# A hybrid encoder layer on one core: transfers of the block products moved to POOL's queue and to column tiles, and the attention's fill respread

## The chip, the cores and the metric

The kernel runs on one core of a Trainium2 chip. The core has TensorE (PE) for matmuls, VectorE (DVE), ScalarE (ACT), GpSimd (POOL) and SyncE (SP), which here only issues transfers. SP, ACT and POOL each have a queue of DMA issues of their own; all transfers are carried out by the same 16 DMA engines. Every engine works off its instructions in order. The metric is the time of one execution on the device in microseconds (us); less is better.

## The reference

One layer of a bidirectional hybrid encoder on a sequence of 512 positions with 2048 channels, in float32, then a final RMSNorm.

```
h = rmsnorm(x, norm_w)
u = h @ w_in            # columns: z_ssm | x,B,C | dt fwd, dt bwd | q_a | kv_a, kr | z_attn | g_ssm | g_attn
# branch A: conv + SiLU on x,B,C; chunked state-space scan forward and backward (chunks of 128,
#           32 heads of 64, 4 groups, state 128); y = (y_fwd + y_bwd + d_skip*x) * silu(z_ssm); group RMSNorm
# branch B: q = rmsnorm(q_a) @ w_uq; k, v = rmsnorm(kv_a) @ w_ukv; rotary part; 16 heads of 128,
#           softmax over all 512 positions; o = (p @ v) * silu(z_attn)
merged = sigmoid(g_ssm) * (y @ w_proj_ssm) + sigmoid(g_attn) * (o @ w_proj_attn)
out = rmsnorm(x + merged @ w_out, final_norm_w)
```

## The kernel before

Each float32 matmul is done as three matmuls of split operands (high and low part, type fp32r): high by high, high by low, low by high. Weights come in chunks of 128 partitions by 1024 (512 KB). A chunk is loaded by SP into one of three buffers `wraw` (`wchunk`, `w_load`, `w_tile("w")`), ACT copies the high part into `wh` (L163, L431), DVE subtracts to get the low part `wl` (L164, L432); `wh` and `wl` have three buffers each.

PE's instructions run in the order in which they are written. On the other engines and queues a scheduler that works from its own cost model orders them; `tc.high_priority(offset=n)` lets what is inside go as if it stood n instructions earlier (`AHEAD` is 60, `LOAD_AHEAD` 160). `tc.keep_in_program_order` pins an instruction behind what was written before it on its engine.

The stages, in order of time:

1. The input is normed and turned; the dt tile and six tiles of `xbc` of group 0 are computed (`xbc_gen`; 16 k-steps of three matmuls each, then a conv of width 4 and SiLU). `h_sums` makes the sums of quarters of h that the block products need, in pool `sx`. `dt_make` makes the time steps, stored to `dt_d`.
2. The products for `z_ssm`, `g_ssm` and `g_attn` (`wz`, `wgs`, `wga`) are block products with seven multiplications in place of eight (`Strassen`). Each of the two column pairs (`pair`) runs P1, P5, P6, P2, P3, P7, P4; a `product` is 4 chunks of 12 matmuls. P1 loads its columns into tiles X, P5 adds column block Y into X (`t2`), P6 uses that sum, P2 adds a further block (`t4`), P4 uses the result; P3 uses Y, P7 a further sum. After a product, hooks load (`L`) or split (`C`) the next operands, which go through `wraw` as `xraw`. The results, through silu or sigmoid, go to scratch (`zs_d`, `gs_d`, `ga_d`).
3. The state-space part, four groups (`ssd_group`). A group loads its BT, CT and four `xs` tiles from scratch, turns them, and runs states, off-diagonal and diagonal blocks. Between its small steps, `gap` runs matmuls of other tiles (xbc of the next group, qkv, z_attn) from a queue, `fill`; one unit of fill is one matmul of 512 columns. Tiles in pool `sw` have eight buffers of tag `t`; `dt64` is the first of them. In the background POOL's queue adds up weight blocks in DRAM (`t_jobs`: T1 and T3 of `wps`, `wpa`).
4. Attention, 16 heads. For a head: `scores` for four blocks of 128 queries, `trans` (turning the probabilities through TensorE), and `pv` for the head before. Between these run `unit`s of fill: first the q, k, v and rotary products of later heads (`qk_gen`, `rope_gen`, `v_gen`), then, queued at the end of head 14, `wps.head()`: P1 and P2 of both column pairs of `wps`. The sums of the attention output that the block products need (`sums(o_d, ...)`, `o_sums`) are DRAM-to-DRAM copies and accumulating transfers on POOL's queue; columns 0 to 1023 at head 12, the others in six steps hung on `wps`'s hooks.
5. The block products `wps` (operands y) and `wpa` (operands o), with summed weights T1 and T3 loaded from DRAM. In `wps` P1 and P2 are done by then, so a pair is P5, P6, P3, P7, P4, and a block of weights is added to X by `t4_alone`. `fetch_ps`/`fetch_pa` load gates (into tag `st`, three buffers) and the partial results of `wps` (`ms`); `done_ps` multiplies and stores `ms_d`, `done_pa` multiplies, adds and turns the result.
6. The last product with `w_out`, the residual, the final norm and the store.

Of the kernel before, what the change touches and what calls it, by code (L numbers as in the profile page):

```python
# [11 lines left out]
F32 = mybir.dt.float32  # L12
# [60 lines left out]
def build(tc, a):  # L73
# [320 lines left out]
    def xbc_gen(g, i, new):  # L394
        p_ = mm("xbc")
        yield from gemm_steps(p_, win(T_XBC + 6 * g + i), h_h, h_l)
        put(xbc_d[g][i], conv_silu(p_, (4 * g + i, 16 + g, 20 + g)[max(0, i - 3)], st("xbc"), new))
# [147 lines left out]
    def product(name, op, chunk, extra=None, pre=None):  # L545

        used.append((used[-1] + 1) % 4)
        bs = [b(name) for b in SETS[used[-1]]]
        for m in range(4):
            raw = chunk(m)  # L550
            h, l = w_split(raw)
            if extra:
                extra(m, raw)
            if pre and m == 2:
                pre()
            for i in range(2):
                for jj in range(2):
                    j = 2 * m + jj
                    xh, xl = op(0, j, i), op(1, j, i)
                    wh, wl = (t[:, jj * 512:(jj + 1) * 512] for t in (h, l))  # L560
                    pe.matmul(bs[i], xh, wh, start=(j == 0), stop=False)  # L561
                    pe.matmul(bs[i], xh, wl, start=False, stop=False)  # L562
                    pe.matmul(bs[i], xl, wh, start=False, stop=(j == 7))  # L563
            yield 12
        product_done()
        return bs

    class Strassen:


        def __init__(self, w, ops, r, done, fetch=None, hooks=None):
            self.w, self.ops, self.r, self.done = w, ops, r, done
            self.fetch, self.hooks = fetch or (lambda t, b: None), hooks or {}

# [41 lines left out]
        def pair(self, cp, headed=False):  # L616

            w, made = self.w, (self.w, cp, "T1") in t_d
            X, Y = [], []
            if not headed:  # L620
                def c1(m):
                    if made:
                        return w_load(w_tile("w"), w, cp, 0, 0, m)
                    X.append(w_load(w_tile("X"), w, cp, 0, 0, m))
                    return X[m]

                p1 = evict((yield from product("P1", self.op("x11"), c1, None if made else
                                               lambda m, raw: w_more(raw, w, cp, 0, 1, m))), "p1")
                self.hook(cp, "P1")
            else:  # L630
                p1 = self.p1[cp]

            def c5(m):
                if made:
                    X.append(t_load(w_tile("X"), w, cp, "T1", m))
# [19 lines left out]
            A = yield from product("P6", self.op("S2"), lambda m: X[m], t4_alone if headed else None)  # L655
# [15 lines left out]
            A = yield from product("P7", self.op("S3"), c7, None, self.pre(2, 2 * cp + 1))  # L671
# [80 lines left out]
    def h_back():  # L752
        h_ops.raws["x21"] = []
        for q in range(2):
# [46 lines left out]
    nc.sync.dma_start(dt64, dt_d)  # L801
# [42 lines left out]
    def ssd_group(g):  # L844
# [29 lines left out]
        nc.sync.dma_start(BT, xbc_d[g][4])  # L874
        nc.sync.dma_start(CT, xbc_d[g][5])
        xss = []
        for ct in range(4):
            xss.append(tmp2("xs"))
            nc.sync.dma_start(xss[ct], xbc_d[g][ct])
# [423 lines left out]
    def fetch_ps(t, b):  # L1303
        fetched[t, b] = st("gate")
        nc.sync.dma_start(fetched[t, b], gs_d[t][b])

    def fetch_pa(t, b):
        fetched[t, b] = st("gate")
        nc.sync.dma_start(fetched[t, b], ga_d[t][b])
        fetched["m", t, b] = sum_tile("ms")  # L1310
        nc.sync.dma_start(fetched["m", t, b], ms_d[t][b])

    def done_ps(t, b, o):
        dve.tensor_mul(o, o, fetched.pop((t, b)))
        nc.sync.dma_start(ms_d[t][b], o)
# [32 lines left out]
    o_half = sums(o_d, slice(1024, 2048))  # L1348

    def o_sums(n):  # L1350
        return lambda: [tc.keep_in_program_order(f()) for f in o_half[n]]
# [11 lines left out]
    def m_room(b):  # L1363
# [6 lines left out]
        (1, "P5"): [L(o_ops, "S1"), o_sums(5)], (1, "P6"): [C(o_ops, "S1"), L(o_ops, "S2")],  # L1370
        (1, "P3"): [C(o_ops, "S2"), L(o_ops, "S4")], (1, "P7"): [C(o_ops, "S4"), L(o_ops, "S3")],
        (1, "P4"): [C(o_ops, "S3"), L(o_ops, "x22")]})
    wpa = Strassen("wpa", o_ops, -1, done_pa, fetch_pa, {
        (0, "P1"): [C(o_ops, "x22")],
        (1, "P1"): [residual], (1, "P6"): [lambda: m_room(2), lambda: m_room(3)], (1, "P2"): [residual, m_load(0)],
        (1, "P3"): [m_split(0), m_load(1)], (1, "P7"): [m_split(1)]})

    for hd in range(AH):
# [4 lines left out]
        unit = 3 if hd < 12 else 2 if hd < AH - 1 else 7  # L1383
        early = unit if hd < AH - 1 else 0
        scores(hd, 0)
        if hd:
            fill.run(early)
            trans(hd - 1, 3)
        fill.run(2 * early)
        scores(hd, 1)  # L1390
        fill.run(3 * early)
        if hd:
            pv(hd - 1)
        if hd == 12:
            for step in sums(o_d, slice(0, 1024)):
                for f in step:
                    f()
        trans(hd, 0)
        scores(hd, 2)
        fill.run(3 * unit)  # L1400
        trans(hd, 1)
        fill.run(2 * unit)
        scores(hd, 3)
        fill.run(3 * unit)
        trans(hd, 2)
        fill.run(3 * unit)
        if hd == AH - 2:
            fill.all()
            close_pool("ap")
# [7 lines left out]
    fill.run(12)  # L1417
    trans(AH - 1, 3)
    fill.run(24)
# [4 lines left out]
    for w in ("S1", "S2"):  # L1424
        y_ops.raws[w] = [cols.tile([P, 1024], F32, tag="X", bufs=4, name="xraw") for q in range(2)]
        for q in range(2):
            nc.sync.dma_start(y_ops.raws[w][q], yn_d[w][:, q * 1024:(q + 1) * 1024])
        C(y_ops, w)()
    fill.all()
    L(y_ops, "S4")()  # L1430
    run(wps.pair(0, True))
# [154 lines left out]
```

## Time and profile before

| | |
|---|---|
| median of 3 runs | 2116.05 us (2115.52 to 2118.23) |
| the profiled execution | 2111.87 us, span 2110.1 us |
| mean granted TensorE clock | 0.975 |
| PE busy | 1979.2 us, 94% of the span |
| DVE, ACT, POOL busy | 70%, 45%, 13% |
| chain that ended last | PE 75%, DVE 10%, DMA 6%, issue 5%, ACT 2%, POOL 1% |
| DMA | 378.56 MB, mean 179 GB/s |

The profile is of one execution. A row of a group has the line, engine, operation, output and inputs, shapes, count, then busy time, mean duration, idle time of the engine before it and what ended it. In a row of waits stand who waited for whom, the sum, how often, and the longest. The granted clock is the share of full speed at which the throttle let TensorE run. Matmuls overlap, so the time of one is read from the distance of their starts.

### The profile page before, as it was taken

How to read it: one execution, taken by the hardware profiler on the slowest of the kernel's cores; microseconds unless marked ns; L12 is line 12 of the kernel's file. 1: busy time of each engine (PE TensorE's matmuls, PEld its weight loads, DVE VectorE, ACT ScalarE, POOL GpSimd, SP SyncE). 2: the span in 40 equal slices, each digit the busy share in tenths (PEclk: the TensorE clock that was granted, in tenths of full speed). 3: DMA queues.
4: the chain of work that ended last, by engine and by line, in shares of the span. 5: the costliest groups of instructions: out<-in, count | busy, mean ns of one | idle time of the engine just before them, and what ended most of it. 6: DMA issues, size and time to landing. Idle time of an engine off the chain costs nothing.

```text
span 2110.1 us, 24659 instructions
## 1 busy us (share of the span) xinstructions
PE 1979.2 (94%) x9074; PEld 1633.7 (77%) x9074; DVE 1467.0 (70%) x1946; ACT 958.6 (45%) x1344; POOL 275.1 (13%) x265
## 2 busy tenths in 40 slices
PE   6989999999989999899899999999988889979998
PEld 5878888888777777787788788888776768857886
DVE  7966676677669589798794767667667877755342
ACT  6444445444444545545555344444444444423232
POOL 0001010010042151342420011200100000000110
PEclk9999999999999999999999999999999999989999
DMA  5468657756646747587564867863659794744332
GB/s 192 143 182 201 168 126 186 191 127 161 169 156 187 216 125 212 189 230 217 156 195 157 240 169 185 226 158 87 166 187 307 247 307 139 268 150 144 109 121 80
DMA packets 170552, 378.56 MB, mean 179 GB/s; under 512 B 15872, under 2 KB 65152, under 8 KB 169856
## 3 DMA queue, kind: packets, MB, share of 16 engines
q1 hardware_dynamic: 113904, 255.11, 37.1%
q0 software_dynamic: 21696, 75.51, 17.8%
q10 hardware_dynamic: 34832, 46.38, 6.2%
q8 instruction: 71, 1.16, 0.2%
q14 instruction: 49, 0.40, 0.1%
HBM read 325.03 MB, written 98.04 MB: 201 GB/s over the span
## 4 chain that ended last, share of the span: by engine, by line
PE 75%; DVE 10%; DMA 6%; issue 5%; ACT 2%; POOL 1%; SPq 0%; ACTq 0%; DVEq 0%; POOLq 0%
PE P L562 11%; PE P L563 11%; PE P L561 11%; PE f L1456 3%; PE f L1454 3%; PE f L1455 3%; PE za L170 2%; PE za L168 2%; PE za L169 2%; PE xbc L168 2%; PE xbc L170 2%; PE xbc L169 2%; DVE sum L980 2%; DVE wl L164 1%; PE pb L1249 1%
## 5 line engine op out<-in xcount | busy, mean ns | idle before, releaser
L432 DVE TENSOR_TENSOR wl<-X,wh 128x1024 fp32r<-128x1024 f32 x144 | 175.5, 1222 | 86.5 <-ACT wh L431 85.9
L164 DVE TENSOR_TENSOR wl<-wraw,wh 128x1024 fp32r<-128x1024 f32 (+2 forms) x148 | 175.4, 1185 | 74.4 <-ACT wh L163 69.2
L431 ACT CAST wh<-X 128x1024 fp32r<-128x1024 f32 x144 | 151.4, 1054 | 162.6 <-PE P L563 145.2
L432 DVE TENSOR_TENSOR wl<-wraw,wh 128x1024 fp32r<-128x1024 f32 x98 | 120.6, 1231 | 148.1 <-ACT wh L431 146.3
L163 ACT CAST wh<-wraw 128x1024 fp32r<-128x1024 f32 (+2 forms) x150 | 145.4, 969 | 164.9 <-PE xbc L169 43.0
L431 ACT CAST wh<-wraw 128x1024 fp32r<-128x1024 f32 x98 | 103.2, 1053 | 203.7 <-PE f L1456 74.9
L561 PE MATMUL P<-wh,h_h 128*128 128x512 f32 x384 | 150.5, 392 | 5.4 <-ACT wh L431 5.4
L168 PE MATMUL xbc<-h_h,wh 128*128 128x512 f32 x384 | 152.3, 397 | 0.0
L562 PE MATMUL P<-wl,h_h 128*128 128x512 f32 x384 | 150.3, 391 | 0.5 <-DVE wl L432 0.5
L170 PE MATMUL xbc<-h_h,wl 128*128 128x512 f32 x384 | 150.3, 391 | 0.4 <-DVE small L827 0.4
L169 PE MATMUL xbc<-h_l,wh 128*128 128x512 f32 x384 | 150.2, 391 | 0.0
L563 PE MATMUL P<-wh,h_l 128*128 128x512 f32 x384 | 150.1, 391 | 0.0
L432 DVE TENSOR_TENSOR wl<-Y,wh 128x1024 fp32r<-128x1024 f32 x64 | 78.3, 1223 | 64.2 <-ACT wh L431 64.1
L561 PE MATMUL P<-wh,S 128*128 128x512 f32 x288 | 112.0, 389 | 0.0
L562 PE MATMUL P<-wl,S 128*128 128x512 f32 x288 | 112.0, 389 | 0.0
L563 PE MATMUL P<-wh,S 128*128 128x512 f32 x288 | 112.0, 389 | 0.0
L431 ACT CAST wh<-Y 128x1024 fp32r<-128x1024 f32 x64 | 67.4, 1054 | 91.2 <-PE P L563 83.3
L170 PE MATMUL za<-h_h,wl 128*128 128x512 f32 x256 | 101.1, 395 | 5.0 <-DVE wl L164 5.0
L168 PE MATMUL za<-h_h,wh 128*128 128x512 f32 x256 | 102.2, 399 | 0.0
L169 PE MATMUL za<-h_l,wh 128*128 128x512 f32 x256 | 100.7, 393 | 0.0
L561 PEld LDWEIGHTS P<-wh,h_h 128*128 128x128 f32 x384 | 72.6, 189 | 21.0 <-ACT wh L431 5.8
L170 PEld LDWEIGHTS xbc<-h_h,wl 128*128 128x128 f32 x384 | 72.5, 189 | 16.3 <-DVE small L827 0.8
(623 smaller groups left out, 5162.4 us busy)
## 6 DMA issues: line engine op xcount, KB each, us to landing
wraw<-wi SPq DMA_DIRECT2D x102, 512.0 KB, 4.2
da<-da_d SPq DMA_DIRECT2D x64, 256.0 KB, 4.3
T_wps<-wps POOLq DMA_DIRECT2D x32, 512.0 KB, 6.2
T_wpa<-wpa POOLq DMA_DIRECT2D x32, 512.0 KB, 9.7
wraw<-wo SPq DMA_DIRECT2D x32, 512.0 KB, 3.4
wraw<-wps SPq DMA_DIRECT2D x24, 512.0 KB, 4.1
wraw<-wpa SPq DMA_DIRECT2D x16, 512.0 KB, 5.2
xbc_d<-xbc ACTq DMA_DIRECT2D x24, 256.0 KB, 2.5
```

Of the source, the lines that this page charges most:

```text
L163: act.copy(h, raw)
L164: (dve if ahead[0] else pool).tensor_sub(l, raw, h.bitcast(F32))
L168: pe.matmul(out, wh, xh, start=start, stop=False)
L169: pe.matmul(out, wh, xl, start=False, stop=False)
L170: pe.matmul(out, wl, xh, start=False, stop=stop)
L431: act.copy(hi_, raw)
L432: dve.tensor_sub(lo_, raw, hi_.bitcast(F32))
L561: pe.matmul(bs[i], xh, wh, start=(j == 0), stop=False)
L562: pe.matmul(bs[i], xh, wl, start=False, stop=False)
L563: pe.matmul(bs[i], xl, wh, start=False, stop=(j == 7))
L1454: pe.matmul(acc, mh, wh, start=(start and k == 0), stop=False)
L1455: pe.matmul(acc, mh, wl, start=False, stop=False)
```

## The change

It has these parts.

- `xbc_gen` may run its conv in its output tile. Five tiles of group 0 run before the block products' pool is opened, the sixth after it and after the issue of the first X loads of `wz` (`first_columns`). The load of operand S3 moves from the hook after P1 to the hook after P5.
- The load of `dt64` is issued `LOAD_AHEAD`, those of BT, CT and `xs` `AHEAD`.
- In `pair`: where sums are made beforehand, P1 takes its weights through X tiles in place of `wraw`, and P7 its T3 through Y tiles. `t4_alone` moves from P6 to P7. For `wps` the first T1 loads are issued before the rest of the fill (`first_columns`).
- A product yields after every 3 matmuls in place of every 12.
- Gates, partial results and their stores (`fetch_ps`, `fetch_pa`, `done_ps`) go on POOL's queue in place of SP's.
- The late `o` sums are split in two halves of 512 columns; one is issued during heads 14 and 15 and before P5, the other on the hooks. Operand loads and splits on the hooks are moved, mostly by one product.
- Attention: `unit` is 2.8 for heads 0 to 13 and 2 for the last two, with what was run too much or too little carried over (`some`); before it was 3, 2 or 7. The head's products are queued in head 14 after `scores(14, 1)`. Operands S1 and S2 go through Y tiles, issued `LOAD_AHEAD`.

The diff, cut; in the heads' loop `fill.run(n)` becomes `some(n)` throughout, and the block `if hd == AH - 2` (close `ap`, load and split x11 and x12, queue `wps.head()`) stands after `scores(hd, 1)` and its fill in place of at the head's end:

```diff
@@ xbc_gen
-        put(xbc_d[g][i], conv_silu(p_, (4 * g + i, 16 + g, 20 + g)[max(0, i - 3)], st("xbc"), new))
+        o = st("xbc")
+        put(xbc_d[g][i], conv_silu(p_, (4 * g + i, 16 + g, 20 + g)[max(0, i - 3)], o, new or (lambda n: o)))
@@ product
-            yield 12
+                    yield 3
@@ Strassen
+            self.made = (w, 0, "T1") in t_d
+            self.ahead = {}
+        def first_columns(self, cp):
+            self.ahead[cp] = [self.columns(w_tile("X"), cp, m) for m in range(4)]
+        def columns(self, t, cp, m):
+            if self.made:
+                return t_load(t, self.w, cp, "T1", m)
+            return w_load(t, self.w, cp, 0, 0, m)
@@ pair
+            X, Y = self.ahead.pop(cp, []), []
+            def column(m):
+                if m == len(X):
+                    X.append(self.columns(w_tile("X"), cp, m))
+                return X[m]
-                    if made:
-                        return w_load(w_tile("w"), w, cp, 0, 0, m)
+                    "P1", self.op("x11"), (lambda m: w_load(w_tile("X"), w, cp, 0, 0, m)) if made else column,
             def c7(m):
-                return t_load(w_tile("w"), w, cp, "T3", m) if made else Y[m]
+                return t_load(w_tile("Y"), w, cp, "T3", m) if made else Y[m]
-            A = yield from product("P6", self.op("S2"), lambda m: X[m], t4_alone if headed else None)
+            A = yield from product("P6", self.op("S2"), lambda m: X[m])
-            A = yield from product("P7", self.op("S3"), c7, None, self.pre(2, 2 * cp + 1))
+            A = yield from product("P7", self.op("S3"), c7, t4_alone if headed else None, self.pre(2, 2 * cp + 1))
@@ before the gates' products
-    for i in range(6):
+    for i in range(5):
         run(xbc_gen(0, (4, 5, 0, 1, 2, 3)[i], sxt))
-    gates[0].hooks = {(0, "P1"): [lambda: h_ops.load("S3")],
-                      (0, "P5"): [lambda: [h_part("S3", 256, q) for q in range(2)]]}
+    gates[0].hooks = {(0, "P5"): [lambda: h_ops.load("S3"), lambda: [h_part("S3", 256, q) for q in range(2)]]}
+    gates[0].first_columns(0)
+    run(xbc_gen(0, 3, None))
@@ state-space part
-    nc.sync.dma_start(dt64, dt_d)
+    with tc.high_priority(offset=LOAD_AHEAD):
+        nc.sync.dma_start(dt64, dt_d)
-        nc.sync.dma_start(BT, xbc_d[g][4])
-        nc.sync.dma_start(CT, xbc_d[g][5])
...
+        with tc.high_priority(offset=AHEAD):
+            nc.sync.dma_start(BT, xbc_d[g][4])
+            nc.sync.dma_start(CT, xbc_d[g][5])
...
@@ fetch_ps, done_ps (fetch_pa in the same way)
-        nc.sync.dma_start(fetched[t, b], gs_d[t][b])
+        pool.dma_start(fetched[t, b], gs_d[t][b])
-        nc.sync.dma_start(ms_d[t][b], o)
+        pool.dma_start(ms_d[t][b], o)
@@ hooks
-    o_half = sums(o_d, slice(1024, 2048))
+    o_late = [sums(o_d, slice(1024 + 512 * i, 1536 + 512 * i)) for i in range(2)]
...
     wps = Strassen("wps", y_ops, -1, done_ps, fetch_ps, {
-        (0, "P5"): [C(y_ops, "S4"), L(y_ops, "S3"), o_sums(0)], (0, "P6"): [C(y_ops, "S3"), L(y_ops, "x22"), o_sums(1)],
-        (0, "P3"): [C(y_ops, "x22"), L(o_ops, "x11"), o_sums(2)],
-        (0, "P7"): [C(o_ops, "x11"), L(o_ops, "x12"), o_sums(3)], (0, "P4"): [C(o_ops, "x12"), o_sums(4)],
...
+        (0, "P5"): [C(y_ops, "S4"), L(y_ops, "S3"), o_sums(5, 0), o_sums(0)],
+        (0, "P6"): [C(y_ops, "S3"), L(y_ops, "x22"), o_sums(1)], (0, "P3"): [C(y_ops, "x22"), o_sums(2)],
+        (0, "P7"): [L(o_ops, "x11"), o_sums(3)], (0, "P4"): [C(o_ops, "x11"), L(o_ops, "x12"), o_sums(4)],
...
@@ attention
-        unit = 3 if hd < 12 else 2 if hd < AH - 1 else 7
-        early = unit if hd < AH - 1 else 0
+        unit = 2.8 if hd < AH - 2 else 2
...
-    fill.run(12)
+    some(8)
     trans(AH - 1, 3)
-    fill.run(24)
+    some(16)
     pv(AH - 1, pb)
@@ after attention
     for w in ("S1", "S2"):
-        y_ops.raws[w] = [cols.tile([P, 1024], F32, tag="X", bufs=4, name="xraw") for q in range(2)]
+        with tc.high_priority(offset=LOAD_AHEAD):
+            y_ops.raws[w] = [cols.tile([P, 1024], F32, tag="Y", bufs=4, name="xraw") for q in range(2)]
...
+        if w == "S1":
+            wps.first_columns(0)
         C(y_ops, w)()
     fill.all()
     L(y_ops, "S4")()
+    o_sums(4, 0)()
```

More of the change, by code (lines that the diff above doesn't have):

```diff
@@ L873, in ssd_group @@
             fill.until(("xbc", g))
-        nc.sync.dma_start(BT, xbc_d[g][4])
-        nc.sync.dma_start(CT, xbc_d[g][5])
         xss = []
-        for ct in range(4):
-            xss.append(tmp2("xs"))
-            nc.sync.dma_start(xss[ct], xbc_d[g][ct])
+        with tc.high_priority(offset=AHEAD):
+            nc.sync.dma_start(BT, xbc_d[g][4])
+            nc.sync.dma_start(CT, xbc_d[g][5])
+            for ct in range(4):
+                xss.append(tmp2("xs"))
+                nc.sync.dma_start(xss[ct], xbc_d[g][ct])
         act.copy(c_h, CT)
@@ L1382, in build @@
         fill.until(("qk", hd))
-        unit = 3 if hd < 12 else 2 if hd < AH - 1 else 7
-        early = unit if hd < AH - 1 else 0
+        unit = 2.8 if hd < AH - 2 else 2
         scores(hd, 0)
         if hd:
-            fill.run(early)
+            some(unit)
             trans(hd - 1, 3)
-        fill.run(2 * early)
+        some(2 * unit)
         scores(hd, 1)
[L1391 to L1406, printed above, removed]
+        some(3 * unit)
         if hd == AH - 2:
             fill.all()
+            owed[0] = 0
             close_pool("ap")
@@ L1416, in build @@
             fill.add("head", wps.head())
-    fill.run(12)
+        if hd:
+            pv(hd - 1)
+        if hd == 12:
+            for step in sums(o_d, slice(0, 1024)):
+                for f in step:
+                    f()
+        trans(hd, 0)
+        if hd == AH - 1:
+            o_sums(2, 0)()
+        scores(hd, 2)
+        some(3 * unit)
+        trans(hd, 1)
+        if hd == AH - 2:
+            o_sums(0, 0)()
+        some(2 * unit)
+        scores(hd, 3)
+        some(3 * unit)
+        trans(hd, 2)
+        some(3 * unit)
+        if hd >= AH - 2:
+            o_sums((1, 3)[hd - AH + 2], 0)()
+    some(8)
     trans(AH - 1, 3)
-    fill.run(24)
+    some(16)
     pv(AH - 1, pb)
```

42 lines of the change are left out of this document (20 added, 22 removed).

## The prediction

> **What bounds the kernel now.** I read the page first, then TensorE's waits, then the table of stretches, then the chain of waits. The page says that TensorE (PE) is the bound, with 131 us idle (2110.1 less 1979.2).
>
> ```profile
> span 2110.1 us, 24659 instructions
> PE 1979.2 (94%) x9074; PEld 1633.7 (77%) x9074; DVE 1467.0 (70%) x1946; ACT 958.6 (45%) x1344; POOL 275.1 (13%) x265
> ```
>
> The waits (engine, line, releaser: total, times, longest) say where. The block products wait for the split of their weights (L431, L432), the state-space part and the attention for single things.
>
> ```profile
> PE P L561 <- ACT wh L431: 44.4, 9, 13.5
> ...
> PE turn L834 <- ACT y L828: 12.1, 4, 4.2
> PE pb L1249 <- DVE pr L1238: 7.9, 1, 7.9
> PE loc L169 <- DVE xw_l L917: 7.6, 5, 2.4
> ...
> PE pb L308 <- DMA dt<-dt_d: 4.9, 1, 4.9
> ```
>
> The table of stretches prices each wait whole, with the slow clock after it. Columns: stretch and length; busy time and count of PE, weight load, VectorE (DVE), ScalarE (ACT), GpSimd (POOL); granted clock; share of the DMA engines; GB/s. The first row is undisturbed: 222 matmuls in 50 us, 0.2252 us each. In the others, length less count times 0.2252 is what the stall costs.
>
> ```profile
> 200.00:250.00 50.00, 50.00 (x222) 41.40 (x221) 36.92 (x35) 23.23 (x27) 3.44 (x4) 1.00 0.53 127
> 108.90:119.80 10.90, 5.02 (x12) 3.58 (x12) 5.74 (x6) 4.44 (x5) 2.78 (x3) 0.69 0.94 357
> 577.00:607.00 30.00, 22.31 (x94) 17.63 (x93) 12.04 (x14) 12.56 (x20) 12.63 (x10) 0.83 0.54 185
> 1518.00:1546.00 28.00, 18.83 (x85) 14.26 (x84) 21.50 (x41) 14.98 (x26) 1.19 (x1) 0.88 0.74 221
> 1594.90:1617.20 22.30, 12.77 (x49) 10.13 (x49) 18.27 (x18) 12.13 (x13) 1.70 (x2) 0.77 0.99 302
> 1629.40:1660.50 31.10, 25.14 (x98) 19.61 (x97) 23.55 (x25) 14.30 (x14) 0.00 (x0) 0.89 0.88 297
> 1693.10:1722.80 29.70, 24.99 (x98) 19.48 (x97) 20.70 (x23) 12.52 (x12) 0.00 (x0) 0.89 0.91 316
> 1722.80:1752.40 29.60, 24.96 (x97) 19.65 (x96) 21.70 (x24) 12.89 (x13) 0.00 (x0) 0.88 0.78 271
> 1865.10:1924.90 59.80, 40.13 (x163) 30.66 (x162) 32.32 (x40) 17.07 (x19) 0.00 (x0) 0.86 0.47 152
> ```
>
> Named in order: A (109, first gate product) 10.9 − 12 × 0.2252 = 8.2. B (577, start of the state-space part) has small matmuls too, so wait plus lost clock: 4.9 + 0.17 × 30 = 10.0. D (1518, hand-over in attention) likewise 7.9 + 0.12 × 28 = 11.3. E (1595, first P5 of wps) 11.3. F (1629, P7 of its first pair) 9.0. G (1693, P7 of its second) 7.6. H (1723, P1 of wpa) 7.8. I (1865, last P7 of wpa) 23.1. Together 88 us, which is about what this change can reach.
>
> The chain (start, length, what) names the releaser of D to I.
>
> ```profile
> 1523.74 7.18 DMA wraw<-wps
> ...
> 1582.09 7.42 DMA o_x<-og
> 1589.57 6.35 DMA xraw<-yn_S
> ...
> 1638.78 1.23 DVE x__13534 L432
> 1640.03 5.00 DMA wraw<-T_wps
> ...
> 1706.77 5.52 DMA wraw<-T_wps
> ...
> 1730.74 6.09 DMA wraw<-wpa
> ...
> 1883.86 5.47 DMA wraw<-T_wpa
> ```
>
> F to I have one form: the weights go through the three `wraw` buffers, the operand loads (`xraw`) and partial results hold them until they are split, and only then does a load of 5 to 6 us start, in sight of PE.
>
> **A: one xbc tile run after the first X loads.** SyncE's (SP's) queue, in order of time:
>
> ```profile
> 95.00 11.25 SPq L462 DMA_DIRECT2D wraw<-wz  x3
> 106.30 2.97 SPq L462 DMA_DIRECT2D X<-wz  x4
> ```
>
> The X loads stood behind a `wraw` load that had to wait for the split of `xraw<-h_S`. That load is now one product later, the X loads are issued ahead, and 48 matmuls of the moved tile (10.8 us) cover them. No instruction is added; the conv works in its output tile. Between 0 and 8.2 I take 8.2, since cover exceeds wait. `S3` is now loaded at P5 and needed at P7, three products or 32 us later; without that cover it would cost a load like F's 5.0.
>
> **B: `dt64` and the group's BT, CT, xs loads issued ahead.**
>
> ```profile
> 571.47 5.77 SPq L160 DMA_DIRECT2D wraw<-wi  x3
> 577.33 0.41 SPq L801 DMA_DIRECT2D dt<-dt_d  x1
> ...
> 579.01 4.21 SPq L879 DMA_DIRECT2D xs<-xbc_d  x4
> ```
>
> The stores of `u` before them, in the view of that tile:
>
> ```profile
> L268 ACTq DMA_DIRECT2D ga_d<-u x2: 326/374/422, 576.2 to 576.7; - x2
> DMA to landing us min/median/max: 2.2/2.6/2.9
> ```
>
> `dt` waits behind three blocked `wraw` loads and goes ahead of them now. What is late next is the fourth `xs` tile: it lies where `u` was, so it can start only when the `u` store has landed, 576.7 + 2.9 = 579.6, against an issue that ended at 583.2. So 3.6 us are sure and 10.0 is the end; I take 6. The price in the queue is that weight loads go behind six loads of 0.4 us issue; PE has chunks split ahead. For groups 1 to 3 the CT load sits ahead of `y` on ACT's queue at one of the four `turn` waits (12.1 us in all): between 0 and 4.2, taken as 2 gained.
>
> **Attention's fill, 2.8 instead of 3 units a slot.** The matmuls stay the same. By the code the queue holds 816 units, runs dry at the end of head 13 in both kernels, and at heads 8 and 12 some 14 units are now forced just before the scores. No row shows that hand-over (cast, subtract, matmul); the nearest is `loc <- xw_l`, at most 2.4. Two of them: between 0 and 4.8 lost, I take 2. A gain is excluded, since the page's idle has no wait of size in attention before 1518.
>
> **D: the head's products moved into head 14.** In the row at 1523.74 the first `wps` chunk waited for `wraw`, and ACT, with `pr` behind it, for the chunk. The new order puts the closing of `ap`, the splits of x11 and x12 and P1 after `scores(14,1)`; in between PE has 12 + 5 + 4 instructions. Which takes `wraw` first is open: the chunk is now issued ahead of the operand loads. Lower end: all 11.3 gone; upper: 3 more than now, since there is less cover. I take 4 gained, below the middle, because the same three buffers serve chunk and operand.
>
> **E: S1, S2 through Y tiles, X loaded ahead, more fill behind pv(15).** Of the head's 192 units, 2 × 11 + 34 + 24 = 80 are run by then, so 112 remain, 25 us of PE instead of some 18, over a chain of 7.42 + 6.35 and splits. Between 5 and 11.3 gained; I take 10.
>
> **F, G, H: T3 through Y, P1 of wpa through X, `t4_alone` from P6 to P7.** Y has four tiles, each free when P3 has split it, up to 10.8 us ahead of P7; a 5.5 us load fits. But then this stretch is full on three sides:
>
> ```profile
> 1597.00:1738.00 141.00, 118.30 (x480) 93.81 (x480) 114.44 (x117) 65.66 (x66) 2.83 (x3) 0.91 0.85 280
> 1581.00:1606.00 25.00, 15.47 (x65) 12.14 (x64) 13.43 (x14) 10.88 (x12) 2.84 (x3) 0.83 0.95 329
> ```
>
> PE needs 480 × 0.2252 = 108.1 us. VectorE has 114.4, less the splits of S1, S2 and of two o operands that leave it, 8 × 1.23 = 9.8, so 104.6. The DMA moves 280 × 141 = 39.5 MB, less about 4.2 MB for eight 512 KB loads that go elsewhere. At row E's 302 GB/s for 0.99 (305 when full) 35.3 MB take 116 us, 7.6 more than PE; at this row's 329 for 0.95 (346) 102 us and nothing. Of 24.4 I leave 7 standing, near the dearer end because the loads come in bursts: 17.4 gained, ends 0 and 24.4.
>
> **I: the same in wpa.** Between 12 (the 13.5 us wait gone, some clock still lost) and 23.1; here the DMA is at 0.47, so nothing is full, and I take 21.
>
> **Gates, stores and partial results on POOL's queue.** Each of the 64 moved DMAs leaves SP's queue, where weights stand behind it, and joins POOL's, where the `o` sums stand. Sum steps that wait for one another hold up a gate behind them.
>
> ```profile
> T_wps<-wps POOLq DMA_DIRECT2D x32, 512.0 KB, 6.2
> ...
> gate<-gs_d SPq DMA_DIRECT2D x16, 256.0 KB, 4.5
> ...
> POOL o_S L1274 <- DMA o_S<-o_x: 21.5, 2, 11.1
> ```
>
> From POOL a transfer lands 1.7 us later by these rows (twice the size). A gate is asked for by the third of four chunks at the latest, 5.4 us ahead, and the sum steps are halved and one product apart. I take 0; ends −3 (SP freed) and the second rival.
>
> **Sum.** −8.2 − 6 − 2 + 2 − 4 − 10 − 17.4 − 21 = −66.6. The profiled execution took 2111.9 (span 2110.1), 4.2 below the median of the runs shown, 2116.05. So 2045 in such an execution, and 2049 for the median.
>
> **A rule weighed against a row.** Short waits cost clock too: here after the 2.4 us wait for `xw_l`, 10 us ran at a mean of 0.83.
>
> ```profile
> 884.00:894.00 10.00, 7.63 (x28) 5.75 (x28) 9.39 (x10) 3.39 (x6) 8.06 (x6) 0.83 0.17 52
> ```
>
> The Trainium skill, TensorE: Matmul & The Clock Gate, section Why this matters for your kernels, puts the limit at idle gaps of about 3 us. By it, remains cut under 3 us would cost only themselves, and the 7 us left in F to H would be about 4, so 2046; the row above, with 2.4 us, disagrees.
>
> **The rivals.**
> First, the wps stretch turns DMA- and VectorE-bound: F to H give half of 17.4, E half of 10, D nothing. 2049 + 8.7 + 5 + 4 = 2067. For it: 0.85 and 114.4 above. Against: 1660 to 1693 already runs without a stall, as no wait in the chain lies there.
> Second, slower: a gate stands on POOL behind a sum step that waits 11.1 us, lands 6.2 later, and VectorE, in order, holds the weight splits behind the multiplication by it. 17.3 − 10.8 (a product) = 6.5 us, and some 3.4 of clock, at 8 product ends of wps: +79, less 66.6, so about 2128. It decides from (66.6 / 8 =) 8.3 us an end. Against: two such waits in all, and half-size steps.
> The Trainium skill, DMA: Bandwidth & Descriptors, section Issuing engine by pattern, gives plain loads and stores to Sync. By that rule, were the 1.7 us exposed at 16 product ends, 27 us would be lost and 2076 result; no run here shows gates on POOL.
> Third, everything goes, D too: 2116 − 88 = 2028.
> Fourth, the change does not do what it says: the T3 loads wait for Y as they waited for `wraw`, F, G and I stay. 2049 + (12 + 21) = 2082. For it: a tile is free only when its splits are done. Against: four tiles of their own.
>
> **How the numbers follow.** Forecast (2037 to 2061) 0.5; first rival 0.2; second 0.06; third 0.12; fourth 0.09; no visible change 0.03. The range 2026 to 2084 leaves out the second, most of the fourth's upper side and the far side of the third, some 2 in 10. A measurement of this kernel tells 0.2% (about 4 us) from no change. Faster 0.91, same 0.03, slower 0.06.
>
> **What would show it.** A: no wait at L561 near 109. B: no wait for `dt_d`, at most a short one for `xs`. D: a wait for wh L431 or `pr` of up to 7 us in head 14. E to I: the 44.4 us row down to 10 or less, `wraw<-T_wpa` gone from the chain, DMA share over 0.9 in wps. It would be wrong if waits on DMA `gate`, or of VectorE for it, appear, if SP's queue blocks on `xs` or X loads, or if D's wait grows.

## The result, and the profile after

The changed kernel takes 2069.66 us (median of 4 runs, 2066.19 to 2073.74); the kernel before, on the same chip, 2117.14. The ratio is 0.9776 with a 95% interval of 0.9756 to 0.9797: 47.5 us faster, where 66.6 were forecast. The time lies inside the range; the likeliest case was 21 us too good, and the first rival's 2067 is nearer than the forecast's 2049, though for another reason than that rival gave.

The page of the profiled execution: the same 9074 matmuls, 96 us of idle time on TensorE instead of 131, and 72 more instructions on POOL.

```profile
span 2066.8 us, 24703 instructions
PE 1970.5 (95%) x9074; PEld 1627.3 (79%) x9074; DVE 1463.1 (71%) x1946; ACT 959.3 (46%) x1344; POOL 315.9 (15%) x337
```

TensorE's waits over the whole span (total, times, longest). Lines have moved: L562 and L563 are the block products, L432 and L433 their weights' split.

```profile
PE turn L848 <- ACT y L842: 10.0, 4, 3.8
...
PE P2b L562 <- ACT wh L432: 6.3, 1, 6.3
PE pb L308 <- DMA dt<-dt_d: 5.4, 1, 5.4
PE P L562 <- ACT wh L432: 5.1, 5, 2.0
...
PE s L1242 <- ACT kh L1197: 3.7, 3, 1.2
PE vp L1179 <- DVE qb L1149: 1.9, 1, 1.9
PE s L1243 <- DVE kl L1198: 1.8, 3, 0.6
```

The 44.4 us that the products waited are 5.1. But dt still takes 5.4 us, P2b has a new 6.3, and the attention's scores wait where they did not. The table of stretches, the first row around P2b, the second the 150 us behind it, the third around the place of I, the last for A:

```profile
1564.00:1600.00 36.00, 29.28 (x119) 23.44 (x118) 21.80 (x22) 17.05 (x18) 2.23 (x4) 0.91 0.83 319
1595.00:1745.00 150.00, 141.95 (x596) 114.34 (x596) 129.49 (x132) 74.56 (x78) 23.25 (x40) 0.97 0.78 270
1840.00:1885.00 45.00, 44.29 (x208) 36.69 (x207) 37.82 (x47) 21.46 (x24) 5.90 (x11) 1.00 0.67 227
108.90:119.80 10.90, 10.90 (x50) 9.01 (x49) 5.89 (x7) 4.35 (x5) 2.12 (x3) 1.00 1.05 304
```

In A, 50 matmuls run where 12 did, and around I TensorE is nearly full, at full clock. The 150 us behind P2b are not: 596 matmuls where at most 150 / 0.2252 = 666 fit. The stretch behind E in the kernel before, for comparison (it begins 94 matmuls further on in TensorE's order):

```profile
1625.00:1775.00 150.00, 134.31 (x550) 107.41 (x549) 118.10 (x119) 66.91 (x68) 0.00 (x0) 0.93 0.70 236
```

46 matmuls more, so some 46 × 0.2252 = 10.4 us won of the 17.4 forecast for F, G and H.

**Two marks split the span.** The first matmul on dt starts the scan, and one `za` matmul that waits for its split ends it. Before, then after (start, length, what, wait ahead of it):

```profile
583.52 0.86 PE L308 MATMUL pb<-cst,dt 128*128 128x128 f32 x4 [4.90 <-DMA dt<-dt_d]
...
1178.89 0.80 PE L170 MATMUL za<-h_h,wl 128*128 128x512 f32 x1 [5.04 <-DVE wl L164]
```

```profile
576.85 1.12 PE L308 MATMUL pb<-cst,dt 128*128 128x128 f32 x4 [5.41 <-DMA dt<-dt_d]
...
1166.65 0.80 PE L170 MATMUL za<-h_h,wl 128*128 128x512 f32 x1 [5.01 <-DVE wl L164]
```

Ahead of the first mark 6.7 us are won, between them 595.4 − 589.8 = 5.6, behind them (2110.1 − 1178.89) − (2066.8 − 1166.65) = 31.1; together the 43.3 between the two spans. The middle one is within chance: ten later kernels, with the same instructions in the same order up to the second mark, take 592.9 to 602.2 us for the scan. What differs is the granted clock. The trace records it as full or half: in the changed kernel TensorE ran 23.2 us of the scan at half clock, in experiment 6, the slowest of the ten, 45.7. Half of that time is, by estimate, what it costs; without it the eleven scans take 577.8 to 582.2 us and the one before 579.4. The scans of the changed kernel and of experiment 6, with the mean clock behind the counts:

```profile
576.85:1166.65 589.80, 555.66 (x2595) 457.96 (x2595) 469.18 (x645) 304.47 (x453) 172.65 (x138) 0.98 0.65 189
```

```profile
575.10:1177.32 602.22, 565.51 (x2595) 465.42 (x2595) 472.34 (x645) 304.58 (x453) 170.73 (x138) 0.96 0.64 186
```

So single traces are compared below by the time from the `za` mark to the end ("the rest": 900.2 us in the changed kernel), beside the medians. The rest differs by chance too. In experiments 3 and 7, whose instructions behind the mark are those of the changed kernel in the same order, it is 896.7 and 894.4 us, and it is the clock again: 40.0 us at half clock in the changed kernel, 33.1 and 27.3 in these two, and without half of that 880.2, 880.1 and 880.6. A rest that is up to 6 us shorter shows nothing by itself. More can be read from its stretches, cut at the same matmuls in every trace (the mark is number 5029 of the 9074 in TensorE's order, P2b begins with 7043; us):

| stretch | before | changed | experiments 3, 7 | gain forecast |
|---|---|---|---|---|
| from the mark to P2b (fill, D) | 405.0 | 411.5 | 410.2, 408.9 | 2 |
| the next 108 matmuls (E) | 36.4 | 33.9 | 33.8, 34.7 | 10 |
| the next 550 (F, G, H) | 150.8 | 139.9 | 136.6, 136.4 | 17.4 |
| from there to the end (I) | 339.0 | 314.9 | 316.1, 314.3 | 21 |

### The profile page after: what moved, and what is told of

The parts are those of the page before. It is cut to its first block, busy times and chain, and to the rows that moved or that the text cites. A ratio compares the mean times of both kernels' runs of the same rounds, so it can differ in the third digit from the quotient of the medians.

```text
span 2066.8 us, 24703 instructions
## 1 busy us (share of the span) xinstructions
PE 1970.5 (95%) x9074; PEld 1627.3 (79%) x9074; DVE 1463.1 (71%) x1946; ACT 959.3 (46%) x1344; POOL 315.9 (15%) x337
## 4 chain that ended last, share of the span: by engine, by line
PE 69%; DVE 11%; DMA 9%; issue 6%; ACT 2%; POOL 1%; SPq 0%; ACTq 0%; DVEq 0%; POOLq 0%
PE P L563 10%; PE P L564 10%; PE P L562 10%; PE f L1485 3%; PE f L1486 3%; PE f L1484 3%; PE za L168 2%; PE za L169 2%; PE za L170 2%; PE xbc L168 2%; PE xbc L169 2%; PE xbc L170 2%; DVE wl L164 2%; DVE sum L995 1%; DMA wraw<-wps 1%
## 5 line engine op out<-in xcount | busy, mean ns | idle before, releaser
L433 DVE TENSOR_TENSOR wl<-X,wh 128x1024 fp32r<-128x1024 f32 x152 | 185.2, 1222 | 81.8 <-ACT wh L432 81.3
L432 ACT CAST wh<-X 128x1024 fp32r<-128x1024 f32 x152 | 159.6, 1053 | 160.0 <-PE P L564 134.6
L433 DVE TENSOR_TENSOR wl<-wraw,wh 128x1024 fp32r<-128x1024 f32 x74 | 91.3, 1233 | 98.5 <-ACT wh L432 98.3
L433 DVE TENSOR_TENSOR wl<-Y,wh 128x1024 fp32r<-128x1024 f32 x80 | 97.8, 1223 | 73.1 <-ACT wh L432 73.0
L563 PE MATMUL P<-wl,h_h 128*128 128x512 f32 x384 | 149.4, 389 | 0.0
L562 PE MATMUL P<-wh,h_h 128*128 128x512 f32 x384 | 149.4, 389 | 0.0
L432 ACT CAST wh<-wraw 128x1024 fp32r<-128x1024 f32 x74 | 78.0, 1054 | 146.0 <-PE f L1486 71.0
L432 ACT CAST wh<-Y 128x1024 fp32r<-128x1024 f32 x80 | 84.2, 1053 | 114.8 <-PE P L564 95.3
L563 PE MATMUL P<-wl,S 128*128 128x512 f32 x288 | 112.4, 390 | 0.6 <-DVE wl L433 0.6
L562 PE MATMUL P<-wh,S 128*128 128x512 f32 x288 | 112.1, 389 | 0.0
L168 PEld LDWEIGHTS xbc<-h_h,wh 128*128 128x128 f32 x384 | 72.6, 189 | 15.0 <-issue 0.2
```

Of the source, the lines that this page charges most:

```text
L168: pe.matmul(out, wh, xh, start=start, stop=False)
L432: act.copy(hi_, raw)
L433: dve.tensor_sub(lo_, raw, hi_.bitcast(F32))
```

## The experiments

All are edits of the changed kernel, which has 2069.66 us and a rest of 900.2 us. The intervals of 4, 5, 8, 11 and 12 lie clear of its own, 0.9756 to 0.9797; those of the others overlap it, and there the rows of the traces have to decide.

**1. The attention's fill, and who waits at 1301, 1387 and 1473 us.**

```diff
-        unit = 2.8 if hd < AH - 2 else 2
+        unit = 3 if hd < 12 else 2
```

> The changed kernel with the attention's fill at three units a call up to head 11 and two from there, instead of 2.8 units a call. Theory: the changed kernel still has some gates' units left over when heads 4, 8 and 12 begin and has to hand them out at once in front of each of these heads; the three hand-overs leave 1.8 us each of gaps on TensorE and half clock behind the last. With three units a call nothing is left over, the gaps at 1301, 1387 and 1473 us are gone, and the time falls by 8 to 10 us, to about 2061. Rival: the units are needed later anyway, heads 13 to 15 run out of fill, and what is won in front is lost there: within 3 us of the changed kernel, with new gaps behind 1490 us.

2064.35 us (ratio to before 0.9743, 0.9718 to 0.9768), rest 893.5. In the changed kernel, TensorE's rows in front of head 4:

```profile
1302.36 0.50 PE L1242 MATMUL s<-kh,qh 128*128 128x512 f32 x1 [1.22 <-ACT kh L1197]
1303.46 0.50 PE L1243 MATMUL s<-kl,qh 128*128 128x512 f32 x1 [0.61 <-DVE kl L1198]
```

With 2.8 units the last step of a head's `qk` work is still in the queue when the head begins, so the cast and the subtraction are issued right in front of the matmuls that read them. With three units the waits at all three places are gone. From the `za` mark to P2b the nine traces with 2.8 units take 408.0 to 411.8 us and the four with three up to head 11 (1, 8, 11, 12) 401.3 to 406.5, by the means 6.6 less. Part of the gain is lost again, not at heads 13 to 15 as the rival said, but at the first product of wps:

```profile
1526.34 0.80 PE L562 MATMUL P<-wh,x__12693 128*128 128x512 f32 x1 [6.34 <-ACT wh L432]
```

It waited 1.34 us for the same in the changed kernel (and 1.66 for the low half). Counted from the mark, the product is reached 7.8 us earlier, but its weights are there only 2.8 us earlier. They stand on SP's queue behind operand loads. By the code these loads' buffers come free only when the fill's last tile is read, and with two units a call in heads 12 and 13 that read (`kh`) comes only 3.0 us earlier.

**2. The burst ahead of P2b.**

```diff
-        if w == "S1":
-            wps.first_columns(0)
```

> The changed kernel without the early request for the four T1 tiles of the second weight matrix (wps), so that these loads are asked for where the product's first step needs them. Theory: P2b's 6.25 us wait at 1581 us is made by eight 512 KB loads that stand ahead of P2b's weights on SP's queue; with four of them behind it the wait falls below 2 us and the time by 6 to 9 us with the half clock, to about 2062. Rival: the queue was bound by bytes in this stretch whatever the order; the same 6 us appear at the next product of wps (P3 or P4, 1590 to 1640 us), and the time stays within 3 us of the changed kernel.

2064.06 us (0.9745, 0.9719 to 0.9770), rest 888.6. SP's queue in the changed kernel (start, length of the issue with its blocking, count):

```profile
1567.56 0.37 SPq L1454 DMA_DIRECT2D xraw<-yn_S  x1
1568.03 2.43 SPq L468 DMA_DIRECT2D X<-T_wps  x4
1570.55 2.12 SPq L1454 DMA_DIRECT2D xraw<-yn_S  x3
1573.67 3.87 SPq L463 DMA_DIRECT2D wraw<-wps  x3
```

Eight 512 KB loads are issued within 5 us, and P2b's weights stand behind them. The chain of waits in the changed kernel, for here and for experiment 5:

```profile
1567.56 6.05 DMA xraw<-yn_S
1573.67 12.47 DMA wraw<-wps
...
1639.53 8.19 DMA xraw<-o_x
...
1705.61 9.32 DMA xraw<-o_S
```

Without the early request the four X loads stand behind P2b's weights, P2b waits 1.5 us, and the stretch from 1564 to 1600 us holds 148 matmuls instead of the 119 above, at no lower rate of bytes:

```profile
1564.00:1600.00 36.00, 33.77 (x148) 27.40 (x147) 25.82 (x27) 16.46 (x17) 3.30 (x6) 1.00 0.89 334
```

The theory holds: the order on the queue made that wait, not the bytes. E's stretch takes 26.5 to 28.5 us in the four kernels without the early request (2, 8, 11, 12) and 33.0 to 35.7 in the nine with it, by the means 6.8 less.

**3. dt asked for earlier.**

```diff
-    dt64 = tmp2("dt64")
+    dt64 = st("dt64")
```

> The changed kernel with the dt tile in one of three already existing store buffers instead of a buffer that is only freed at the end of the gate stage, so that its load is asked for some products earlier, ahead of the wi loads on SP's queue. Theory: the 5.4 us wait for dt at the start of the scan's stage is the load's place behind three wi loads that themselves wait for VectorE; asked for earlier, dt is there, the wait goes, and the time falls by 4 to 6 us, to about 2065. Rival: BT, CT and xs, still behind the same three loads, are waited for instead and the time stays within 2 us; or the gates, with two store buffers instead of three, lose what the start of the scan wins.

2071.95 us (0.9783, 0.9757 to 0.9808): no gain. The hoisted load of the changed kernel had not moved at all on SP's queue,

```profile
564.30 5.77 SPq L160 DMA_DIRECT2D wraw<-wi  x3
570.16 0.41 SPq L815 DMA_DIRECT2D dt<-dt_d  x1
```

and the same order was there before. With another tile dt does move ahead of these loads (it is issued at 107.9 us) and its wait is gone, but the next two take its place, as the rival said:

```profile
577.12 0.63 PE L872 MATMUL pb<-cst,BT 128*128 128x128 f32 x4 [2.92 <-DMA BT<-xbc_d]
580.85 1.11 PE L872 MATMUL pb<-cst,xs 128*128 128x128 f32 x4 [3.10 <-ACT dec L321]
```

**4. T3 back into the wraw buffers.**

```diff
-                return t_load(w_tile("Y"), w, cp, "T3", m) if made else Y[m]
+                return t_load(w_tile("w"), w, cp, "T3", m) if made else Y[m]
```

> The changed kernel with one line put back: the T3 tiles of the made weight matrices go through the three wraw buffers again instead of the four Y tiles. Theory: the four Y tiles are what lets P7's weights arrive before P7 begins, in wps and in wm (24 us of 47 won at P7 of wm's second pair by itself, some 11 more in wps); put back, the time rises by 25 to 40 us, to 2095 to 2110. Rival: the spread of the weight sums over column tiles is what freed DMA time and VectorE, the tiles only follow; then the time rises by less than 10 us.

2104.60 us (0.9943, 0.9921 to 0.9965): 34.9 of the 47.5 us hang on this line. The 13.5 us wait of I is back, and SP's queue shows why:

```profile
1884.96 0.80 PE L562 MATMUL P<-wh,S__14251 128*128 128x512 f32 x1 [13.50 <-ACT wh L432]
```

```profile
1851.40 25.44 SPq L443 DMA_DIRECT2D xraw<-m_d  x3
1878.26 8.24 SPq L468 DMA_DIRECT2D wraw<-T_wpa  x2
```

The T3 loads share three buffers with operand loads that block for 25 us.

**5. The four transfers back on SP's queue.**

```diff
-        pool.dma_start(fetched[t, b], gs_d[t][b])
+        nc.sync.dma_start(fetched[t, b], gs_d[t][b])
...
-        pool.dma_start(ms_d[t][b], o)
+        nc.sync.dma_start(ms_d[t][b], o)
```

(and the two loads of `fetch_pa` in the same way)

> The changed kernel with the gates' loads and the partial results' stores and loads (the four transfers of the product's done step) on SP's queue again, nothing else undone. Theory: the queue they are issued on is worth nothing by itself, since SP is held by free buffers and the 16 engines by bytes; the time stays within 3 us of the changed kernel (2064 to 2075), with the waits of wps's third and seventh products where they are. Rival: SP's queue, on which a gate that waits for its buffer stands ahead of X and Y loads, was a third or more of what the last two matrices won (35 us); then P of wps and wm waits 10 us or more longer, to 2080 or above.

2057.72 us (0.9727, 0.9705 to 0.9750), rest 890.3: the theory fell, on the other side than its rival. By the medians this part of the change costs 11.9 us. The same 150 us behind P2b:

```profile
1600.00:1750.00 150.00, 148.03 (x642) 121.09 (x641) 135.89 (x138) 79.12 (x82) 0.00 (x0) 0.99 0.79 266
```

642 matmuls instead of 596, or of 611 in experiments 3 and 7, which is worth 7 to 10 us, with VectorE busier than in the slower kernel: VectorE is not the bound. The 550 matmuls of F to H take 135.9 to 139.9 us in the six traces with the four transfers on POOL (changed, 1, 2, 3, 7, 8) and 129.5 to 130.9 in the three with them on SP (5, 11, 12), by the means 7.1 less. The DMA engines move as much, but other bytes. POOL's issues in the changed kernel, in order of time:

```profile
1569.20 0.60 POOL L1330 DMA_DIRECT2D ms_d<-p  x1 [30.24 <-DVE p L1329]
...
1600.87 0.54 POOL L1330 DMA_DIRECT2D ms_d<-p  x1 [28.87 <-DVE p L1329]
...
1606.01 0.54 POOL L1289 DMA_DIRECT2D o_S<-o_S  x1
...
1610.01 0.87 POOL L1292 DMA_DIRECT2D o_S<-o_x  x1 [2.93 <-DMA o_S<-o_S]
...
1657.29 0.92 POOL L1292 DMA_DIRECT2D o_S<-o_x  x1
...
1675.90 0.87 POOL L1292 DMA_DIRECT2D o_S<-o_x  x1 [3.41 <-DMA o_S<-o_S]
```

and with the transfers on SP, the last of them:

```profile
1571.67 0.82 POOL L1292 DMA_DIRECT2D o_S<-o_x  x1 [12.41 <-DMA o_x<-og]
...
1596.09 0.81 POOL L1292 DMA_DIRECT2D o_S<-o_x  x1 [5.32 <-DMA o_S<-o_S]
```

A store of a partial result cannot go before VectorE has made it. On POOL, which issues in order, everything behind it waits too, here 30.2 and 28.9 us: the sums of attention's output end at 1676 us instead of 1596, and move their bytes while the products of wps load weights. The chain above points the same way: two of its three longest transfers are operands of the next matrix (`o_x`, `o_S`) in this very time.

**6. The bytes of wps's gates taken away.**

```diff
-        fetched[t, b] = st("gate")
-        pool.dma_start(fetched[t, b], gs_d[t][b])
+        fetched[t, b] = cst[:, 0:SEQ]
```

> The changed kernel without the loads of the gates of wps's products (32 loads of 256 KB; a constant tile stands in for the gate, so the output's gate values are left out). Theory: the 9 us of gaps that remain between 1619 and 1735 us are bytes: the 16 DMA engines are 94 to 100% busy there; with 16 x 256 KB less in each half of the stretch the loads of weights land earlier and at least half of the gaps go: 2060 to 2065. Rival: the gaps are the chain load, ACT's cast, DVE's subtraction behind the released buffer, whatever the bytes; the gaps at 1621, 1636, 1648 and 1711 to 1717 us stay as long, and the time within 3 us.

2067.65 us (0.9767, 0.9743 to 0.9792). (By the profile the gate loads left out are 16, not 32.) In the stretch:

```profile
1602.00:1752.00 150.00, 143.66 (x618) 116.33 (x617) 132.40 (x134) 77.25 (x80) 15.74 (x26) 0.99 0.72 242
```

22 matmuls more than the changed kernel, but only 7 more than experiments 3 and 7; rest 891.4. The median moves by 2.0, inside the rival's 3 and inside the interval. With 242 GB/s instead of 270 most of the gaps are still there, so the amount of bytes is not shown to make them; the stores alone, without wps's gates on POOL, leave them.

**7. The first part undone.**

```diff
-    for i in range(5):
+    for i in range(6):
...
-    gates[0].hooks = {(0, "P5"): [lambda: h_ops.load("S3"), lambda: [h_part("S3", 256, q) for q in range(2)]]}
+    gates[0].hooks = {(0, "P1"): [lambda: h_ops.load("S3")],
+                      (0, "P5"): [lambda: [h_part("S3", 256, q) for q in range(2)]]}
...
-    gates[0].first_columns(0)
-    run(xbc_gen(0, 3, None))
```

> The changed kernel with the first part undone alone: six convolutions ahead of the gate stage again, no early request for its first columns, the S3 load back at the first product's hook. Theory: this part took the 7 us of waits and half clock at 109 us, and nothing else; undone, these come back at the same place and the time rises by 6 to 9 us, to 2076 to 2079. Rival: the work moved (one convolution) only shifts the wait; then the time stays within 3 us.

2080.14 us (0.9826, 0.9792 to 0.9860), 10.5 more, 1.5 beyond the theory's upper end, with the wait where it was:

```profile
114.37 0.80 PE L562 MATMUL P<-wh,h_h 128*128 128x512 f32 x1 [5.42 <-ACT wh L432]
```

In its trace the first mark is 6.3 us later, which is this part's price; what the median has beyond that is within the differences between runs (2072.60 to 2083.87 here).

**8. Edits 1 and 2 together.**

> The changed kernel with both edits that each won alone: the fill at three units a call up to head 11 and two from there, and no early request for wps's first T1 columns. If the two are independent, as their places (1301 to 1476 us; 1581 us) say, both wins of 5.5 us add up: 2058 to 2060. Rival: with the fill's even pace the first product of wps already waits 6.3 us for its weights (it did with the even fill alone), and with the burst gone the wait at 1581 us goes but this one stays, so that 2062 to 2065 is all there is.

2056.36 us (0.9718, 0.9695 to 0.9741), 13.3 less, rest 881.4. The means by stretch above are 6.6 for the fill and 6.8 for the burst: they add up. The first product's wait is there too (6.7 us), as the rival said, but it costs nothing beyond what it cost in experiment 1.

**9 and 10. Which transfer holds POOL's queue.** One puts back the store's line of experiment 5 alone, the other the three loads.

> The changed kernel with one line put back: the stores of the partial results (ms) on SP's queue, the gates' loads still on POOL's. Theory: POOL's queue goes in program order, and a store that waits for the product's end holds the sums of attention's output (o_S, copies and additions of 512 KB each) that stand behind it; these move from 1570-1596 us to 1606-1641 us, onto the loads of wps's weights, and that is the 9 us of gaps left between 1619 and 1717 us. With the stores elsewhere the sums run at 1570 to 1600 us again and the gaps go: 2056 to 2061, as with all four transfers on SP. Rival: the gates' loads hold them as well, or it is the software queue's own slowness with small transfers; then the time stays within 3 us of the changed kernel (2067 to 2072).

> The counterpart: the gates' and partial results' loads on SP's queue, the stores still on POOL's. Theory: the stores still hold the o_S sums, so the gaps between 1619 and 1717 us stay and the time is within 3 us of the changed kernel, 2067 to 2072. Rival: the loads are what matters; the gaps go and the time falls to 2056 to 2061.

2068.37 us (0.9773, 0.9756 to 0.9791) and 2066.57 us (0.9760, 0.9742 to 0.9778): neither is told from the changed kernel by its time. The stretch of each, stores on SP first:

```profile
1608.00:1758.00 150.00, 144.56 (x625) 116.41 (x624) 132.52 (x134) 77.15 (x81) 11.58 (x20) 1.00 0.77 267
```

```profile
1601.00:1751.00 150.00, 145.01 (x628) 116.55 (x627) 133.64 (x135) 77.12 (x81) 14.69 (x24) 1.00 0.79 270
```

29 and 32 matmuls more than the changed kernel, but 14 and 17 more than experiments 3 and 7, of the 31 that all four bring over these; rests 895.0 and 892.8. My claim that the stores alone hold the sums fell. With the stores on SP, a gate's load stands in the same place: it waits for its buffer, which the same VectorE instruction frees.

```profile
1578.56 0.60 POOL L1320 DMA_DIRECT2D gate<-gs_d  x1 [29.02 <-DVE p L1329]
1579.14 0.55 POOL L1289 DMA_DIRECT2D o_S<-o_S  x1
```

Either kind of transfer, put in program order ahead of the sums, holds them; only with both away do they run early. The last sum, stores on SP first, then loads:

```profile
1664.02 0.86 POOL L1292 DMA_DIRECT2D o_S<-o_x  x1 [5.80 <-DMA o_S<-o_S]
```

```profile
1677.99 0.86 POOL L1292 DMA_DIRECT2D o_S<-o_x  x1 [4.31 <-DMA o_S<-o_S]
```

So the sums are nearly as late as in the changed kernel, and yet about half of the lost matmuls are back in each. By this stretch the lateness of the sums is at most half of what this part costs, and the other half is not explained. With the stores on SP, P2b even waited 8.3 us; the first sums ran beside its loads then, which may be the reason.

**11 and 12. The three edits (1, 2 and 5), and a fill that ends earlier.** The second has `unit = 3 if hd < 12 else 2.3 if hd < 14 else 2`.

> Three edits together: the fill at three units a call up to head 11 and two from there, no early request for wps's first T1 columns, all four transfers on SP's queue. If the three wins are independent (13 us for the first two together, 12 for the third): 2043 to 2048. Rival: with the T1 columns asked for later, the freed queue is busy with the gates just when they are asked for, and the gaps between 1610 and 1720 us come back: 2052 or above.

> As the three edits together, but the fill at 2.3 units in heads 12 and 13 instead of 2, so that the last of it is handed out before head 14 begins. Theory: the first product of wps waits 6.3 to 6.7 us for its weights with two units because its operands' loads can only be split once the fill's last tile is read, and that end stayed at 1515 us while the product came 5 us earlier; with the end of the fill 4 us earlier the wait falls to 2 to 3 us: 2039 to 2045, some 4 us below the three edits with two units. Rival: the heads without fill lose on TensorE's side what the product wins: within 2 us of the three edits.

2053.31 us (0.9697, 0.9675 to 0.9720) and 2050.03 us (0.9689, 0.9675 to 0.9704); both beat both kernels, the second by 66 us against before and 19.6 against the changed one. In the trace of the first the three wins do add up: without the share of half clock its rest is 863.1, 17.1 less than the changed kernel's, against 3.4 + 4.1 + 8.4 = 15.9 for experiments 1, 2 and 5, and the rival's gaps are not there (640 matmuls in the 150 us from 1585). Its median is yet 5 us above my 2048, 16.4 less than the changed kernel's, where the three alone have 5.3 + 5.6 + 11.9 = 22.8. Its five runs reach from 2044.67 us, at a mean granted clock of 0.988, to 2059.86, at 0.983; the profiled one is the fastest of them. The second: P1's wait falls from 6.6 to 4.8 us, not to 2 to 3, and the 3.3 us between the medians are less than these intervals can tell.

## Why the prediction was right or wrong

- **A, 8.2 forecast:** right. 6.7 won at the first mark; undone alone, 6.3 lost there again.
- **B and the scan's loads, 8 forecast:** wrong. The step that failed is "`dt` ... goes ahead of them now". The request was hoisted, but the queue kept its order, because the tile lies in a buffer that comes free only behind the gate stage: with another tile (experiment 3) the load does go ahead. Experiment 3 adds that even 5 us of dt would have bought nothing, with BT and `dec` 3 us behind. The 5.6 us that this pair of traces shows between the marks is less than the scan differs from run to run.
- **Attention's fill, 2 lost:** mis-sized. I counted heads 8 and 12; there are three hand-overs (head 4 too) with two waits each, 5.5 us, and half clock behind the last. Taken away, 6.6 us come back up to P2b by the means, 5.3 in the median, net of what P1 then waits.
- **D, 4 gained, and E, 10 gained:** up to P2b, fill and D together lost 3.9 to 6.5 us where 2 were to be won. With 6.6 of that put down to the fill, D brought 0 to 3 (P1 waits 3.0 us where `pr` cost 7.9). E brought 1.7 to 2.6 of its 10, and 9.1 without the burst: the 6.25 us wait at P2b took most back. The step that failed is "112 units remain": the cover was counted in TensorE's work, the queue ahead of P2b's weights was not.
- **F, G, H, 17.4 gained:** 10.9, and 14.2 and 14.4 in the traces of experiments 3 and 7. The 7 us left standing were 12 to 16 in that stretch ((666 − 611) and (666 − 596) × 0.2252). I priced them by all bytes of the stretch; some 7 us of them go with the gates and stores on POOL's queue (experiment 5), which my sum had at nothing.
- **I, 21 gained:** right, with 22.9 to 24.7; no wait is left there, and experiment 4 brings all of it back.
- **Gates and stores on POOL's queue, 0:** the failed step that matters most, 7 us in the traces and 12 in the medians. I asked who holds up a gate; the question was whom a gate and a store hold up. The second rival had the right queue and the wrong direction: in the stretch VectorE waits for no gate. That the sums are held is seen in the rows; that this is what costs the time is argued, and by experiments 9 and 10 it can be half of it at most.

Behind the second mark the forecast's terms are −50.4; the changed kernel's trace has −31.1, those of experiments 3 and 7 −34.5 and −36.8. Experiments 1, 2 and 5 account for the difference of 14 to 19 us: fill (6.6), burst (6.8) and POOL's queue (7.1), by the means over all traces. So the time came out as near as it did because A and I hold, and F to H in part; the wrong steps at B, the fill, E and POOL's queue all go the same way.

The Trainium skill, DMA: Bandwidth & Descriptors, section Issuing engine by pattern, gives plain loads and stores to Sync, and the runs agree: gates land 7.9 us after the issue from POOL and 4.8 from SP. But what experiment 5 wins is not that latency, for which VectorE waits 2.2 us in all; the rows point to the order on POOL's queue, about which the rule says nothing.

The first rival's 2067 came close by its halves of E and F to H, but VectorE as the bound is excluded by experiment 5, where it does more in the same time. The amount of bytes alone is not it either: experiment 5 moves them at 266 GB/s and has few gaps, experiment 6 moves 242 and has most of them.

**What stays open:** what the 7 to 12 us of POOL's queue are made of: the sums' bytes at the wrong time, the operands that wait for them (`xraw<-o_S`, 9.3 us in the chain), or something of the transfers themselves, since half comes back with the sums still late. Open too is why the same code runs at half clock longer in one run than in the next.

## What to carry to other kernels

Before a transfer is moved to another queue, list what stands behind it there in program order: a store that waits for a result holds all of that, for as long as the result takes (30 us here). Asking for a load earlier moves nothing while its buffer is the thing that is late, and what is asked for earlier stands ahead of something; look at the queue's rows, in order of time, on both sides of the edit. Where a stage differs by 10 us from run to run with the same code, look at the granted clock first; compare single traces in stretches cut at the same instructions, and use every trace that has the same code there.

## What had not been expected of the hardware

Waits of 2 us and less cost clock, and not always. In the changed kernel the pairs of waits of 1.22 and 0.61 us at 1301 and 1387 us were followed by full clock, the same pair at 1473 by a stretch at 0.83; 1.96 and 0.95 us at 1648 by 0.72:

```profile
1472.00:1482.00 10.00, 8.17 (x30) 6.08 (x29) 3.99 (x9) 2.68 (x5) 0.00 (x0) 0.83 0.23 66
1646.00:1658.00 12.00, 9.10 (x27) 6.71 (x26) 8.81 (x11) 5.98 (x6) 2.32 (x5) 0.72 0.96 358
```

The scan, the same code in each of the runs compared, takes from 589.8 to 602.2 us between the two marks, while the first mark agrees within 2 us. Most of that is the clock, 23.2 to 45.7 us at half; why the same waits bring half clock in one run and not in the next, nothing in the runs here says.
